# Hybrid encoder layer, convolution stages: own bytes for the raw memory weights, second-stage loads written first, a third buffer in the last stage

## The chip, the cores and the metric

The kernel runs on one core of a Trainium2 chip. The metric is the device time of one execution in microseconds (us), the median of several runs. TensorE runs the matrix products; VectorE, ScalarE and GpSimd do the element-wise work; SyncE (SP) issues nearly all transfers between DRAM and the core's on-chip memory, in one queue, which 16 DMA engines work off.

## What is computed

One layer on two sequences (4096 and 1024 rows of 1024 values) that share their weights:

```python
h = rms_norm(x, norm_in)
z = h @ w_in                      # columns for the three branches and a gate
y_hy  = x0 * (fft_conv(x1 * v, filter) + skip * x1 * v)
y_att = dilated_attention(q, k, v, rel_bias)      # 6 heads, 3 window sizes
y_mem = memory_attention(qm, mem, mem_norm, w_mem_kv, ...)   # 4 heads, 256 memory rows
x + (concat(y_hy, y_att, y_mem) * silu(gate)) @ w_out
```

The change touches two parts of it: the long convolution `fft_conv`, and the preparation of `w_mem_kv`, the weights from which the keys and values of the memory rows are made.

## The kernel before

Products are run as three half-precision products each (`mm3`, lines 275 to 282: high by high, high by low, low by high), so each weight is scaled by a power of two and split into a high and a low part (`wsplit`, lines 235 to 264: load, multiply by a gain on GpSimd, largest magnitude on VectorE, high part on ScalarE, low part on VectorE).

`phases` (line 1586) first runs the projection for the convolution branch (`hyena_proj`, its weights in `wh`, its products in `zh`). Then it weaves two streams. `dense` makes the queries, keys and values row block by row block (`qkv`, products `z` from `wA` and a row block `hA`, three at a time) and then the gates. `side` runs `long_conv` for both sequences, then `memory_kv`, then the attention. Each generator yields an estimated cost, and `weave` takes the next piece from the stream that has spent less; a bare yield such as `IDLE_2` lets the dense stream run for so long. `K_C` = 1.35 scales the costs of `long_conv`, and `IDLE_2` is 9000 and 16000 (ns) for the two sequences.

The order of TensorE's instructions is the order in which the program writes them. On the other engines and on the queue of SP the scheduler places each instruction by its estimate of when it is ready, and among ready ones by a priority that rises in the order of writing, with the dense stream (3 million) ahead of the side stream (4 million). On each engine the result is one list that is worked off in order.

`long_conv` (line 1231) is a Fourier convolution in three stages, each in a pool of its own:

- `pc1`: the scaled signal is split into `s16` from pieces `sl` of 1024 columns (lines 1248 to 1258); `conv_stage1` transposes 64 (16) blocks of it on TensorE (line 1282), multiplies by a constant matrix and stores the result to `as_d` in DRAM (line 1298).
- `pmw`, for the first sequence only: `memory_weights` (line 503) loads the four parts of `w_mem_kv` in two pairs, into two buffers of 4 KB a partition, and writes the split weights `wm` into a pool that stays. It has no matmul. Its products with the memory rows come in `memory_kv`, some 580 us later.
- `pc2`: `conv_stage2` loads batches of four groups (`fk` from the filter's spectrum `as_k`, `fa` from `as_d`, constant matrices `mt`; the first batch of the first sequence is one group), makes spectra (line 1335 and line 1352), multiplies them, and transforms back (line 1376) into `bs` in DRAM.
- `pc3`: `conv_stage3` loads eight blocks at a time from `bs` into `bt` (line 1403, two buffers; for the first sequence eight batches in two transfers of 768 KB each, for the second two batches), runs 24 small matmuls for each of three channel groups (line 1420), and ScalarE writes them to `big` (line 1425).

A pool takes the bytes above the pools that are open. When it closes, the next pool takes the same bytes, and its tiles wait until the tiles that lay there are no longer in use. So before the change `pc1`, `pmw`, `pc2` and `pc3` all begin at the same byte.

Of the kernel before, what the change touches and what calls it, by code (L numbers as in the profile page):

```python
# [12 lines left out]
F32 = mybir.dt.float32  # L13
F32R = mybir.dt.float32r
F16 = mybir.dt.float16
I32 = mybir.dt.int32
AF = mybir.ActivationFunctionType
ALU = mybir.AluOpType
# [4 lines left out]
P = 128  # L23
# [115 lines left out]
K_C, IDLE_1, IDLE_2, IDLE_3, IDLE_M = 1.35, (34000, 28000), (9000, 16000), 18000, 40000  # L139
# [39 lines left out]
class Layer:  # L179
# [1051 lines left out]
    def long_conv(self, ps, i, mpool):  # L1231
        nc, x = self.nc, self.x
        L = self.seqs[i][1]
        NB, q = self.groups_of(i)
        nb = L // 512
        m = self.const.tile([P, 3, 4], F32, name=f"lm{i}")
        nc.vector.tensor_reduce(out=m[:, :, 0:1], in_=self.smax[i], axis=AX.X, op=ALU.max)
        nc.vector.tensor_scalar_max(m[:, :, 0:1], m[:, :, 0:1], 1e-30)
        self.pow2(m[:, :, 1:2], m[:, :, 0:1])
        nc.vector.tensor_scalar_mul(m[:, :, 1:2], m[:, :, 1:2], 2.0)  # L1240
        nc.vector.reciprocal(m[:, :, 2:3], m[:, :, 1:2])
        nc.vector.scalar_tensor_tensor(
            out=m[:, :, 3:4], in0=m[:, :, 1:2], scalar=1.0 / (128.0 * NB * 0.5 / 16.0), in1=self.rn[i][:, 1:4].unsqueeze(2),
            op0=ALU.mult, op1=ALU.mult,
        )
        with self.pool("pc1") as sub:
            s16 = sub.tile([P, 3, 2 * L], F16, name="s16", bufs=1)
            for t0 in range(0, L, 1024):
                for c in range(3):
                    sv = s16[:, c].rearrange("p (a l) -> p a l", a=2)  # L1250
                    t = sub.tile([P, 1024], F32, tag="sl", name="sl", bufs=2)
                    self.ld(t, self.s_d[i][c, :, t0:t0 + 1024])
                    nc.scalar.activation(out=sv[:, 0, t0:t0 + 1024], in_=t, func=AF.Identity, scale=m[:, c, 2:3])
                    nc.vector.scalar_tensor_tensor(
                        out=sv[:, 1, t0:t0 + 1024], in0=t, scalar=m[:, c, 2:3], in1=sv[:, 0, t0:t0 + 1024],
                        op0=ALU.mult, op1=ALU.subtract,
                    )
                    yield 800
            yield IDLE_1[i]
            yield from self.conv_stage1(sub, ps, i, s16)  # L1260
        if mpool is not None:
            with self.pool("pmw") as wpool:
                self.memory_weights(mpool, wpool)
        yield IDLE_2[i]
        with self.pool("pc2") as sub:
            yield from self.conv_stage2(sub, ps, i)
        yield IDLE_3
        with self.pool("pc3") as sub:
            big = sub.tile([P, 3, L], F32, name="big", bufs=1)
            yield from self.conv_stage3(sub, ps, i, big, m)  # L1270
# [28 lines left out]

        yield from pipe(NB, (2, stage1), (0, turn))  # L1300

    def conv_stage2(self, pool, ps, i):

        nc, x = self.nc, self.x
        NB, q = self.groups_of(i)
# [9 lines left out]
        def load(nb):  # L1315
            g0, n = batches[nb]
            w = loaded[nb] = {}
            w["k"] = self.load_stage(pool, i, self.as_d[i, "k"], g0, n, "fk2", 4)
            w["x"] = self.load_stage(pool, i, self.as_d[i], g0, n, "fa2", 4)
            w["m"] = pool.tile([P, 4, 2, 2, P], F16, tag="mt", name="mt", bufs=MT)  # L1320
            self.ld(w["m"][:, :n], x[f"mats{i}"][g0:g0 + n].rearrange("g p (m a b) -> p g m a b", m=2, a=2))

        load(0)

        def spectrum(g):
            nb, j = where[g]
            if j == 0 and nb + 1 < len(batches):
                load(nb + 1)
            w = loaded[nb]
            kr = slice(0, 64) if (q == 1 and g in (0, 64)) else slice(0, P)  # L1330
            kt = kts[g] = pool.tile([P, 2, DH], F32, tag="kt", name="kt", bufs=3)
            kp = ps.tile([P, 512], F32, tag="e", name="kp", bufs=2)
            for nn, (ml, ah) in enumerate(PASSES):
                hs = slice(ah * DH, (ah + 1) * DH)
                nc.tensor.matmul(
                    kp[:, :DH], w["m"][kr, j, 0, ml, :], w["k"][kr, j, hs], start=(nn == 0), stop=(nn == 2)
                )
            yield 490
            for a, b in ((0, 0), (0, 1), (1, 1)):
                nc.scalar.activation(  # L1340
                    out=kt[64 * b:64 * b + 64, a], in_=kp[64 * a:64 * a + 64, :DH], func=AF.Identity,
                    scale=rn[64 * a:64 * a + 64, 0:1],
                )
# [51 lines left out]
    def conv_stage3(self, pool, ps, i, out, m):  # L1395
        nc = self.nc
        L = self.seqs[i][1]
        NB, q = self.groups_of(i)
        bs = self.bs[i]
        nbat = 8  # L1400

        def load(n0):
            bt = pool.tile([P, nbat, 768], F16, tag="bt", name="bt", bufs=2)
            nk = 64 // q
            for ri in range(2):
                for l in range(q):
                    p0, r0 = 64 * ri + nk * l, 2 * NB * l + NB * ri + n0
                    self.ld(bt[p0:p0 + nk], bs[r0:r0 + nbat, 0:nk].rearrange("n k c -> k n c"))
            return bt

        nxt = load(0)
        for n0 in range(0, NB, nbat):
            bt = nxt
            if n0 + nbat < NB:
                nxt = load(n0 + nbat)
            for c in range(3):
                o = ps.tile([P, nbat, 64], F32, tag="f", name="o", bufs=3)
                for jn in range(nbat):
                    for nn, (dh, ch) in enumerate(((0, 0), (0, 1), (1, 0))):
                        nc.tensor.matmul(  # L1420
                            o[:, jn, :], bt[:, jn, dh * DH + c * P:dh * DH + (c + 1) * P], self.cinv[i][:, ch, :],
                            start=(nn == 0), stop=(nn == 2),
                        )
                yield 24 * 44
                nc.scalar.activation(
                    out=out[:, c, :L].rearrange("p (n t) -> p t n", t=NB)[:, n0:n0 + nbat, :], in_=o,
                    func=AF.Identity, scale=m[:, c, 3:4],
                )
        self.st(self.cv[i].rearrange("c p l -> p c l"), out[:, :, :L])
# [251 lines left out]
```

## Time and profile before

| | |
|---|---|
| median of the runs | 3072.31 us (3069.44 to 3073.78, 3 runs) |
| profiled execution | 3067.02 us, of it 3065.2 us span |
| TensorE busy | 2775.0 us, 91% of the span |
| VectorE busy | 2052.3 us, 67% |
| ScalarE busy | 1663.4 us, 54% |
| GpSimd busy | 1259.7 us, 41% |
| DMA | 610.38 MB, mean 199 GB/s |

The span runs from the first to the last instruction. A busy TensorE is not one at its peak, since overlapping matmuls count in full. In a row of the timeline the brackets hold the idle time of the engine ahead of the instruction and what ended it; an `x24` folds 24 alike instructions.

### The profile page before, as it was taken

The page shows a single profiled execution, that of the slowest core. Times are in us where ns is not written, and L with a number is a line of the kernel's source. Part 1 is how long each engine was busy: PE and PEld are TensorE (multiplying, and loading weights), DVE is VectorE, ACT ScalarE, POOL GpSimd, SP SyncE. Part 2 cuts the span into 40 slices and gives each one's busy share as a digit, 9 for nine tenths or more (in the row PEclk, how much of TensorE's full clock was granted, in tenths as well). Part 3 has the DMA queues.
Part 4 walks back from the last instruction along what each step waited for, and adds up shares of the span by engine and source line. Part 5 has one row for each costly group of instructions (what it writes and reads, how often), then busy time and mean ns, then how long its engine had stood idle before and what let it go on. Part 6 is the DMA issues. An engine that isn't in the chain of part 4 may idle for free. (4 is left out here: it accounts for less than half of the span.)

```text
span 3065.2 us, 55390 instructions
## 1 busy us (share of the span) xinstructions
PE 2775.0 (91%) x19620; PEld 1725.3 (56%) x19620; DVE 2052.3 (67%) x5237; ACT 1663.4 (54%) x3149; POOL 1259.7 (41%) x1534
## 2 busy tenths in 40 slices
PE   5998989888959998999999998989899899999999
PEld 2444444333625544544456666666666665778787
DVE  7777888787648882364567666767677665665663
ACT  5666666334738884464366565656566554232321
POOL 2336777232126661142133233333344344555551
PEclk9999999999979999999999999999999999999999
DMA  7554444555559969697499999999998989777762
GB/s 224 175 151 151 155 148 146 155 164 190 208 167 230 246 200 209 214 202 176 110 222 265 216 202 203 225 210 191 210 219 197 202 172 315 250 239 252 236 223 97
DMA packets 761855, 610.38 MB, mean 199 GB/s; under 512 B 514958, under 2 KB 702262, under 8 KB 758122
## 3 DMA queue, kind: packets, MB, share of 16 engines
q1 hardware_dynamic: 761578, 606.84, 75.2%
q8 instruction: 155, 2.54, 0.3%
q14 instruction: 122, 1.00, 0.1%
HBM read 289.08 MB, written 199.92 MB: 160 GB/s over the span
## 5 line engine op out<-in xcount | busy, mean ns | idle before, releaser
L1063 ACT ACTIVATE pt<-pt,nm 128x256 f32<-128x256 f32 (+2 forms) x880 | 350.0, 472 | 182.6 <-DVE nm L1061 171.4
L279 PE MATMUL z<-wA,hA 128*128 128x512 f16 (+1 forms) x960 | 352.5, 367 | 18.1 <-ACT rw L440 14.5
L280 PE MATMUL z<-wA,hA 128*128 128x512 f16 (+1 forms) x960 | 352.7, 367 | 0.0
L281 PE MATMUL z<-wA,hA 128*128 128x512 f16 (+1 forms) x960 | 352.5, 367 | 0.0
L1051 DVE CUSTOM_DVE_ANT_0 pt<-s,tab,lsc 128x256 f32<-128x256 f32 (+1 forms) x672 | 278.9, 449 | 100.9 <-PE s L1047 89.5
L279 PE MATMUL zh<-hB,wh 128*128 128x512 f16 x720 | 280.1, 389 | 25.0 <-ACT zb L877 24.8
L280 PE MATMUL zh<-hB,wh 128*128 128x512 f16 x720 | 279.5, 388 | 1.5 <-DVE hB L384 1.5
L281 PE MATMUL zh<-hB,wh 128*128 128x512 f16 x720 | 279.3, 388 | 0.0
L279 PE MATMUL oo<-wo,mhi 128*128 128x512 f32 x640 | 257.3, 402 | 10.1 <-DVE xr L1557 5.0
L281 PE MATMUL oo<-wo,mlo 128*128 128x512 f32 x640 | 253.8, 397 | 1.3 <-POOL mlo L1536 1.3
L280 PE MATMUL oo<-wo,mhi 128*128 128x512 f32 x640 | 253.7, 396 | 0.0
L1079 POOL CAST hl<-pt 128x256 f16<-128x256 f32 (+1 forms) x212 | 102.8, 499 | 359.4 <-ACT pt L1063 288.3
L279 PE MATMUL zg<-hG,wg 128*128 128x512 f16 x640 | 246.9, 386 | 0.8 <-DVE vr L475 0.7
L280 PE MATMUL zg<-hG,wg 128*128 128x512 f16 x640 | 246.8, 386 | 0.0
L281 PE MATMUL zg<-hG,wg 128*128 128x512 f16 x640 | 246.1, 385 | 0.0
L1099 DVE TENSOR_TENSOR tl<-tt,th 128x512 f16<-128x512 f32 (+1 forms) x280 | 187.8, 673 | 59.9 <-ACT th L1098 58.4
L1098 ACT ACTIVATE th<-tt 128x512 f16<-128x512 f32 (+1 forms) x280 | 159.4, 574 | 102.5 <-PE yp L1120 50.3
L1094 PE MATMUL tt<-ident,pt 128*128 128x128 f32 x1088 | 173.4, 282 | 35.6 <-DVE tl L1099 25.8
L1044 PE MATMUL s<-kT,qT 128*128 128x256 f16 (+2 forms) x720 | 165.6, 261 | 38.2 <-DVE mx L1051 33.9
L1080 POOL TENSOR_TENSOR hl<-pt,hl 128x256 f16<-128x256 f32 (+1 forms) x212 | 190.4, 906 | 6.4
L891 DVE SCALAR_TENSOR_TENSOR u<-zb,cw,u 128x512 f32<-128x512 f32 (+2 forms) x180 | 167.3, 933 | 33.4 <-ACT u L887 29.9
L1094 PEld LDWEIGHTS tt<-ident,pt 128*128 128x128 f32 x1088 | 132.1, 145 | 71.3 <-issue 31.3
(303 smaller groups left out, 7167.7 us busy)
## 6 DMA issues: line engine op xcount, KB each, us to landing
y<-yc SPq DMA_DIRECT2D x120, 198.0 KB, 4.5
yc<-y SPq DMA_DIRECT2D x112, 198.0 KB, 2.8
xt<-in_x SPq DMA_DIRECT2D x40, 512.0 KB, 4.7
hts<-hB SPq DMA_DIRECT2D x10, 2048.0 KB, 6.6
hA<-hts SPq DMA_DIRECT2D x40, 512.0 KB, 5.4
rows<-rw SPq DMA_DIRECT2D x40, 512.0 KB, 4.3
hG<-hts SPq DMA_DIRECT2D x10, 2048.0 KB
gt<-go SPq DMA_DIRECT2D x80, 256.0 KB, 3.3
```

What stands on the lines that cost most here:

```text
L279: nc.tensor.matmul(out, pick_l(lh, k), pick_r(rh, k), start=(k == 0), stop=False)
L280: nc.tensor.matmul(out, pick_l(lh, k), pick_r(rl, k), start=False, stop=False)
L281: nc.tensor.matmul(out, pick_l(ll, k), pick_r(rh, k), start=False, stop=(k == n - 1))
L891: nc.vector.scalar_tensor_tensor(out=u[:, :w], in0=zb[:, c0 + d:c1 + d], scalar=cw[:, j, tap:tap + 1], in1=u[:, :w], op0=ALU.mult, op1=ALU ...
L1044: nc.tensor.matmul(s[:, a, :W], g["qT"][:, h, qs], g["kT"][:, h, kc:kc + W], start=True, stop=False,)
L1051: nc.vector.tensor_tensor_reduce(out=pt[:, h, :W], in0=s[:, a, :W], in1=zero.to_broadcast([P, NMEM]) if mem else tb[:, h, t0:t0 + W], scal ...
L1063: nc.scalar.activation(out=pt[:, h, :W], in_=pt[:, h, :W], func=AF.Exp, bias=nm[:, h:h + 1])
L1079: nc.gpsimd.tensor_copy(hl[:, 0, :, c], src)
L1080: nc.gpsimd.tensor_tensor(out=hl[:, 1, :, c], in0=src, in1=hl[:, 0, :, c], op=ALU.subtract)
L1094: nc.tensor.transpose(tt[:, a, ci, :], pt[:, 2 * pr + a, w0:w0 + P], self.ident)
L1098: nc.scalar.activation(out=th[:, :, :n], in_=tt[:, :, :n], func=AF.Copy)
L1099: nc.vector.tensor_tensor(out=tl[:, :, :n], in0=tt[:, :, :n], in1=th[:, :, :n], op=ALU.subtract)
```

## The change

`pmw` is opened ahead of `pc1` and closed after `pc2`, so the buffers of the raw memory weights lie below both, and `pc1` and `pc2` share bytes among themselves alone. `conv_stage2` loads its first batch, then calls `memory_weights`, then yields `IDLE_2`; before, the weights and the yield stood ahead of the pool. The costs that are yielded, and their order, are the same. `conv_stage3` has three buffers `bt` and loads two batches before the first product and batch n + 2 at batch n.

```diff
-        with self.pool("pc1") as sub:
-            s16 = sub.tile([P, 3, 2 * L], F16, name="s16", bufs=1)
...
-            yield IDLE_1[i]
-            yield from self.conv_stage1(sub, ps, i, s16)
-        if mpool is not None:
-            with self.pool("pmw") as wpool:
-                self.memory_weights(mpool, wpool)
-        yield IDLE_2[i]
-        with self.pool("pc2") as sub:
-            yield from self.conv_stage2(sub, ps, i)
+        with self.pool("pmw") as wpool:
+            with self.pool("pc1") as sub:
+                s16 = sub.tile([P, 3, 2 * L], F16, name="s16", bufs=1)
...
+                yield IDLE_1[i]
+                yield from self.conv_stage1(sub, ps, i, s16)
+            with self.pool("pc2") as sub:
+                yield from self.conv_stage2(
+                    sub, ps, i, IDLE_2[i], (lambda: self.memory_weights(mpool, wpool)) if mpool is not None else None
+                )
...
-    def conv_stage2(self, pool, ps, i):
+    def conv_stage2(self, pool, ps, i, idle, aside):
...
         load(0)
+        if aside is not None:
+            aside()
+        yield idle
...
-            bt = pool.tile([P, nbat, 768], F16, tag="bt", name="bt", bufs=2)
+            bt = pool.tile([P, nbat, 768], F16, tag="bt", name="bt", bufs=3)
...
-        nxt = load(0)
+        bts = [load(n0) for n0 in range(0, min(2 * nbat, NB), nbat)]
         for n0 in range(0, NB, nbat):
-            bt = nxt
-            if n0 + nbat < NB:
-                nxt = load(n0 + nbat)
+            bt = bts.pop(0)
+            if n0 + 2 * nbat < NB:
+                bts.append(load(n0 + 2 * nbat))
```

## Rows read from the trace of the kernel before

**Rows 1.** Waits of TensorE, 873:935 and 1165:1250: us in total, times, longest.
```profile
PE kp L1335 <- DMA mt<-in_mats: 33.8, 2, 28.9
...
PE o L1420 <- DMA bt<-bs: 15.6, 4, 5.8
```

**Rows 2.** Timeline of TensorE: start, duration, instruction, idle before it and its releaser.
```profile
902.08 1.14 PE L1335 MATMUL kp<-fk,mt 64*128 64x384 f16 x3 [28.86 <-DMA mt<-in_mats]
...
912.04 1.14 PE L1335 MATMUL kp<-fk,mt 128*128 128x384 f16 x3 [4.96 <-DMA mt<-in_mats]
...
916.95 0.38 PE L279 MATMUL z<-wA,hA 128*128 128x512 f16 x1
```

**Rows 3.** Stretches: length, busy time (instructions) of five engines, TensorE clock, DMA share, GB/s.
```profile
872.85:902.08 29.23, 0.38 (x2) 0.00 (x1) 18.78 (x57) 5.79 (x7) 7.43 (x6) 0.54 0.29 91
902.08:916.95 14.87, 9.91 (x27) 3.22 (x28) 3.06 (x6) 3.98 (x7) 1.90 (x2) 0.52 1.10 242
916.95:919.22 2.27, 2.27 (x14) 1.18 (x12) 1.10 (x3) 2.00 (x4) 0.99 (x1) 1.00 1.10 213
```

**Rows 4.** Timeline of the DMA issues on SP, 858:935.
```profile
861.41 0.32 SPq L195 DMA_DIRECT2D as_d<-av  x1
861.82 1.70 SPq L192 DMA_DIRECT2D ws<-in_w_mem_kv  x2
...
898.62 0.49 SPq L192 DMA_DIRECT2D fk<-as_k  x1
...
900.42 1.29 SPq L192 DMA_DIRECT2D fk<-as_k  x2
```

**Rows 5.** Timeline of VectorE and of ScalarE in the memory weights' chain.
```profile
871.34 1.22 DVE L249 TENSOR_REDUCE peak<-ws 128x1 f32<-128x1024 f32 x1 [9.88 <-POOL ws L248]
...
894.64 2.19 ACT L260 ACTIVATE wm<-ws,wsa 128x1024 f16<-128x1024 f32 x2 [11.96 <-DVE wsa L257]
```

**Rows 6.** DMA issues, 840:870: count, size, median us to landing.
```profile
vrows<-vr SPq DMA_DIRECT2D x1, 193.5 KB, 6.1
```

**Rows 7.** A setup load on SP's timeline; the first projection's products (durations, first, last).
```profile
19.41 1.93 SPq L192 DMA_DIRECT2D gains<-in_att_q_norm  x1
...
L281 PE MATMUL zh<-hB,wh x720: 377/379/634, 40.5 to 697.6; 128*128 128x512 f16 x180
```

**Rows 8.** Stretches ahead of stage 1 of the first sequence.
```profile
700.00:770.00 70.00, 58.71 (x281) 28.13 (x280) 52.98 (x117) 30.76 (x42) 16.22 (x18) 0.95 0.57 185
...
705.00:710.00 5.00, 4.50 (x21) 1.96 (x20) 4.26 (x19) 1.15 (x1) 1.04 (x1) 1.00 0.00 0
```

**Rows 9.** Last split of s16 on VectorE's timeline; the transposes of s16 (first start).
```profile
767.58 1.28 DVE L1254 SCALAR_TENSOR_TENSOR s<-sl,lm,s 128x1024 f16<-128x1024 f32 x1
...
L1282 PE MATMUL tp<-ident,s x240: 218/251/314, 772.5 to 1303.7; 128*128 128x128 f16 x120
```

**Rows 10.** Timeline of the DMA issues on SP: second sequence's second stage.
```profile
1306.75 5.44 SPq L192 DMA_DIRECT2D fk<-as_k  x8
```

**Rows 11.** Timeline of TensorE in stage 3, a restart after a wait.
```profile
1218.28 1.44 PE L1420 MATMUL o<-cinv,bt 128*128 128x64 f16 x24 [4.41 <-DMA bt<-bs]
...
1223.36 0.99 PE L1420 MATMUL o<-cinv,bt 128*128 128x64 f16 x24
```

**Rows 12.** Stretches of 5 us in stage 3 of the first sequence.
```profile
1165.00:1170.00 5.00, 5.00 (x25) 2.29 (x24) 0.82 (x1) 2.14 (x3) 0.26 (x1) 1.00 1.13 203
1170.00:1175.00 5.00, 5.00 (x69) 3.24 (x67) 1.59 (x2) 2.50 (x4) 0.87 (x2) 1.00 0.46 142
1175.00:1180.00 5.00, 5.00 (x70) 3.37 (x69) 3.10 (x9) 3.63 (x6) 1.15 (x2) 1.00 0.57 188
...
1205.00:1210.00 5.00, 5.00 (x80) 3.64 (x79) 3.37 (x9) 3.59 (x7) 0.00 (x0) 1.00 0.48 101
```

**Rows 13.** Timeline of the DMA issues on SP in stage 3.
```profile
1161.89 0.33 SPq L192 DMA_DIRECT2D hA<-hts  x1
...
1176.79 1.26 SPq L192 DMA_DIRECT2D bt<-bs  x2
```

More of the change, by code (lines that the diff above doesn't have):

```diff
@@ L1245, in long_conv @@
         )
-        with self.pool("pc1") as sub:
-            s16 = sub.tile([P, 3, 2 * L], F16, name="s16", bufs=1)
[L1248 to L1258, printed above, removed]
-            yield IDLE_1[i]
-            yield from self.conv_stage1(sub, ps, i, s16)
-        if mpool is not None:
-            with self.pool("pmw") as wpool:
-                self.memory_weights(mpool, wpool)
-        yield IDLE_2[i]
-        with self.pool("pc2") as sub:
-            yield from self.conv_stage2(sub, ps, i)
+        with self.pool("pmw") as wpool:
+            with self.pool("pc1") as sub:
+                s16 = sub.tile([P, 3, 2 * L], F16, name="s16", bufs=1)
+                for t0 in range(0, L, 1024):
+                    for c in range(3):
+                        sv = s16[:, c].rearrange("p (a l) -> p a l", a=2)
+                        t = sub.tile([P, 1024], F32, tag="sl", name="sl", bufs=2)
+                        self.ld(t, self.s_d[i][c, :, t0:t0 + 1024])
+                        nc.scalar.activation(out=sv[:, 0, t0:t0 + 1024], in_=t, func=AF.Identity, scale=m[:, c, 2:3])
+                        nc.vector.scalar_tensor_tensor(
+                            out=sv[:, 1, t0:t0 + 1024], in0=t, scalar=m[:, c, 2:3], in1=sv[:, 0, t0:t0 + 1024],
+                            op0=ALU.mult, op1=ALU.subtract,
+                        )
+                        yield 800
+                yield IDLE_1[i]
[3 more added lines that the diff above has]
+                    sub, ps, i, IDLE_2[i], (lambda: self.memory_weights(mpool, wpool)) if mpool is not None else None
+                )
         yield IDLE_3
```

## The prediction

> **What bounds the kernel now.** I read part 2 of the page first: TensorE is at nine tenths in nearly every one of the 40 slices, and the dips that lie in one stage each are what a local edit can fill. Then the waits of TensorE in the two stretches that the diff touches [rows 1]: 33.8 us for the constant matrices of the first transform's second stage, in two waits, and 15.6 us for its third stage, in four. TensorE runs in the order in which the program is written, and the edit writes no matmul in another place, since the memory weights have none. So the chain of TensorE is the same list of instructions before and after, and only the waits in it can change.
>
> The first dip, read in the timeline of TensorE [rows 2]: the last dense matmul starts at 872.85, the first spectrum matmul of stage 2 at 902.08 after 28.86 us of idle. Another 4.96 us follow ahead of the second spectrum. The stretch table [rows 3] shows that nothing was busy for its own sake: the DMA engines were at 0.29 in the gap. From 902.08 to 916.95 the granted clock was 0.52, that is mostly the lower level of 1.2 GHz, after an idle of 28.9 us. The queue of the DMA issues [rows 4] says why: the memory weights are loaded at 861.82, as soon as stage 1 has left the bytes, and the first load of stage 2 (fk) is issued at 898.62, after the last split of the weights. Their chain runs through DMA, GpSimd, VectorE and ScalarE one after another, with waits of 9.88 us on VectorE and 11.96 us on ScalarE in it [rows 5]. Stage 2 waits for bytes, not for data.
>
> **Part 1: bytes of their own for the raw memory weights.** After the edit `fk`, `fa` and `mt` stand on the bytes of stage 1 only. Two things hold them then: the last reading of `s16`, over by 861.82, when the weights were let onto the same bytes, and the last store of stage 1, issued at 861.41 [rows 4]. The nearest row for that store's landing is 6.1 us, from a store of `vrows` in the same stretch [rows 6], so `fa` can be issued at about 867.5. TensorE wants it at about 874.2, the matrices at 873.1.
>
> What goes: 28.86 us of idle. Then the stretch of 14.87 us [rows 3]: it holds nine groups of three matmuls (five on the spectra, four dense). At the full clock four such groups take 2.27 us, the last row of [rows 3], so the nine take about 5.1. The loss there is 9.8 us, 4.96 of it the second wait and 4.8 the low clock. Together 38.7 us.
>
> What is next late there: the load of the second batch. In the trace before, its first DMA is issued at 900.42 and the spectrum that needs it starts at 912.04: 11.6 us [rows 2, 4]. Now it can be issued from about 861 to 868, so it lands between 873 and 880; it is wanted at 875.4 (matrices) to 876.5 (product). I take 1.5 us of wait; the bounds are nothing and the whole 9.8 us of before.
>
> **Where the memory weights go.** Engines other than TensorE, and the DMA queue, take what is ready. The gains of the setup are issued at 19.41, though they are written behind a yield of 50 us of TensorE's time [rows 7]. So the weights, once they wait for no bytes of stage 1, will go as soon as the bytes of the first pool are left: its weights are last read at 697.6 [rows 7]. At 705 to 710 the DMA share was 0.00 [rows 8], so the first pair loads free. The work itself is most of the 18.8 us of VectorE, 5.8 of ScalarE and 7.4 of GpSimd in the old gap [rows 3]. It then lies beside the preparation of `s16`, in a stretch where VectorE has 17 of 70 us free and TensorE idles 11 [rows 8]. `s16` is complete at 768.9 and first read at 772.5 [rows 9], a cover of 3.6 us. The second pair of loads (1 MB) must share the DMA engines with the loads of `s16`, and GpSimd, VectorE and ScalarE work in order, so an eviction of a dense product can stand behind a weight that has not arrived. I take 2 us on TensorE. Bounds: below nothing there is no reason for a gain; above, see the last rival.
>
> **Part 2: the load of stage 2 is written ahead of its yield.** For the second sequence this is all that changes, and it is worth nothing: its loads went out at 1306.75 already, as soon as its stage 1 was over [rows 10], because the yield orders TensorE alone. Nor does writing them ahead of the weights matter by itself: what held them was the bytes.
>
> **Part 3: the third buffer of stage 3.** The second sequence has two batches and loads both ahead in either version: nothing. For the first, four waits sum to 15.6 us [rows 1], and after the longer ones TensorE restarts at the lower clock: from 1218.28 to 1223.36 it needs 5.08 us [rows 11] for 24 small matmuls and 9 dense ones, which take 0.70 + 9 x 0.2155 = 2.64 at the full clock. That is 2.4 us; for three such restarts I take 6. So 21.5 us are lost there. But the third buffer gives back only what the DMA engines left unused. While they carried `bt` they were at a share of 1.13 and 203 GB/s [rows 12]; a batch (two DMAs of 768 KB) takes 7.75 us of them at that rate, and TensorE eats one in 6 to 7 us. They fell to 0.46 and 0.57 at 1170 to 1180, when both buffers were full and the next load waited for 1176.79 [rows 12, 13], and to 0.48 at 1205 to 1210. Set against 1.13 that is 5 x (0.67 + 0.56 + 0.65) / 1.13 = 8.3 us of transfer. So the last batch arrives some 8 us sooner, and TensorE keeps about 13 of the 21.5. I take 8; the bounds are 3 (if the dense stream's block `hA`, issued at 1161.89 [rows 13] behind six instead of four transfers, comes late for the next tile) and 21.5.
>
> The Trainium skill, "DMA: Bandwidth & Descriptors", section "Bandwidth", measures 341 GB/s for a transfer of 1 MB. By that figure a batch would take an estimated 4.6 us, the stage would be TensorE's and all 21.5 us would come back; the trace's 203 GB/s, with descriptors of 1.5 KB, speaks against it.
>
> **Sum.** -38.7 + 1.5 + 2 - 8 = -43.2 us. The profiled execution took 3067.02 us (span 3065.2) and would take 3024; it lies 5.3 us below the median of the runs, 3072.31, and I carry the difference to that median: 3029. It should pass to the end whole, since TensorE's list behind 916.95 is the same and its loads are set off by its own progress. That orders on the other engines shift a little everywhere is an uncertainty of some 10 us either way that no row prices.
>
> **Rivals.**
> - The weights do not move ahead but stay at about 862 to 900, now beside stage 2. For: they are written there, with the lowest rank of the two streams. Against: the gains at 19.41. ScalarE is then the bound: at the full rate of stage 2 it is busy 2.00 of 2.27 us [rows 3], so the weights' activations (most of 5.8 us) come on top, and a wait of up to 11.96 us at its head [rows 5] stops the evictions behind it. Then 38.7 shrinks to 21 to 33, and with 8 less 1.5 the whole gain is 27 to 39: 3033 to 3045, about 3038.
> - Stage 3 gives back everything. For: the first two batches were in, and the engines at half their share, before TensorE had emptied a buffer [rows 12]. Against: the share of 1.13 ahead of that. 38.7 - 1.5 - 2 + 21.5 = 56.7: 3016.
> - The stall moves instead of going, and the kernel is slower: the weights' chain, now ahead of stage 1, holds up `s16`. If all of the chain's engine time (18.8 + 5.8 + 7.4) and its two long waits (21.8) came in front of `s16`, the first transpose would be late by 53.8 - 3.6 = 50.2 us, with 4.8 of low clock behind it: 55 against a gain of 45, so 3082. It decides from the point where `s16` is complete later than about 817 instead of 768.9. For: VectorE is three quarters busy there and works in order. Against: the weights rank below `s16`, and most of that work lies on different engines at the same time.
> - The same with part of it (s16 complete between 808 and 820), or loads of stage 2 still held by something I do not see: no change, about 3070.
>
> **How the numbers follow.** Forecast 0.60, weights beside stage 2 0.20, all of stage 3 0.10, no change 0.05, slower 0.05. The likeliest gives 3029. The range must leave out no more than 0.2: 3012 (nothing new late, all of stage 3 back, -60) to 3052 (weights in the way at their worst, 3 us from stage 3, and something over). Faster than 0.2% (about what a measurement of this kernel tells from no change, 6 us) 0.90, within it 0.05, slower 0.05.
>
> **What would show it.** Right: no wait of the first spectrum over 3 us, at about 873; a granted clock of 1.00 through it; `ws<-in_w_mem_kv` issued near 700 and not at 861; waits of stage 3 down to some 10 us with the DMA share near 1.1 throughout; stage 2 to the end the same length. Wrong: the first transpose of stage 1 later than 776; waits of ScalarE for the weights' scales inside stage 2; stage 3 without a wait, or with as many.

## The result, and the profile after

The changed kernel takes 3045.19 us in the median (3033.4 to 3053.22, 6 runs), the kernel before 3070.88 us beside it (3063.98 to 3080.76). The ratio is 0.9914, with a 95% interval of 0.9894 to 0.9935: by the ratio 26.4 us less (20 to 33 by the interval; the medians differ by 25.7), where 43 were forecast. A second series of runs gives 0.9906 (0.9884 to 0.9929). The profiled execution of the changed kernel took 3053.22 us (span 3051.3), the slowest of its six.

Line numbers from 1254 on are shifted by up to 3 against before (transposes L1281, spectrum L1337, product L1354, stage 3 L1422).

The waits of TensorE for transfers at the beginning of stage 2 and in stage 3 of the changed kernel (columns as in [rows 1]):

```profile
PE kp L1337 <- DMA mt<-in_mats: 3.9, 1, 3.9
...
PE o L1422 <- DMA bt<-bs: 8.2, 3, 4.3
```

And its timeline, the first spectra and product (columns as in [rows 2]):

```profile
885.68 0.66 PE L1337 MATMUL kp<-fk,mt 64*128 64x384 f16 x3
887.02 0.66 PE L1354 MATMUL xp<-fa,mt 64*128 64x384 f16 x3
892.32 1.14 PE L1337 MATMUL kp<-fk,mt 128*128 128x384 f16 x3 [3.88 <-DMA mt<-in_mats]
...
897.44 0.38 PE L279 MATMUL z<-wA,hA 128*128 128x512 f16 x1
```

The wait of 28.86 us [rows 2] is gone; the second spectrum still waits. But the first spectrum starts at 885.68 and not at the 873 at which the dense work was through before. The stretch table (columns as in [rows 3]) shows what the second wait leaves behind it: a clock of 0.76, a mixture of the two levels, with the DMA engines now at a share of 1.08. The nine groups that took 14.87 us before [rows 3] take 11.8 here, from 885.68 to 897.44.

```profile
885.00:895.00 10.00, 6.12 (x24) 2.15 (x23) 5.31 (x8) 4.74 (x8) 3.44 (x3) 0.76 1.08 296
```

SP's queue, start and duration of each issue, against [rows 4]:

```profile
716.42 1.02 SPq L192 DMA_DIRECT2D ws<-in_w_mem_kv  x2
...
750.45 3.42 SPq L192 DMA_DIRECT2D ws<-in_w_mem_kv  x2
...
873.94 0.32 SPq L195 DMA_DIRECT2D as_d<-av  x1
874.35 0.48 SPq L192 DMA_DIRECT2D fk<-as_k  x1
878.71 0.46 SPq L192 DMA_DIRECT2D fa<-as_d  x1
879.22 0.58 SPq L192 DMA_DIRECT2D mt<-in_mats  x1
879.85 1.29 SPq L192 DMA_DIRECT2D fk<-as_k  x2
881.18 1.27 SPq L192 DMA_DIRECT2D fa<-as_d  x2
```

The raw weights moved ahead as forecast, from 861.82 to 716.42 and 750.45. The first `fk` follows stage 1's last store by 0.4 us, so nothing holds the bytes any more. Then the queue stands still for 4 us: the first `fa` reads what that store writes, and while it waits to be issued, `mt` and the whole second batch stand behind it, though of these only the second `fa` reads what stage 1 wrote.

What the weights did where they are now, in the stretch from 720 to 780: first the kernel before,

```profile
720.00:780.00 60.00, 49.87 (x248) 24.57 (x247) 48.95 (x113) 29.52 (x43) 13.37 (x14) 0.97 0.62 201
```

then the changed one,

```profile
720.00:780.00 60.00, 49.40 (x234) 23.42 (x232) 58.28 (x123) 28.90 (x37) 21.05 (x15) 0.94 0.67 214
```

then a kernel without the weights' work (`e_no_weights`, below):

```profile
720.00:780.00 60.00, 49.26 (x229) 23.43 (x228) 48.10 (x110) 26.94 (x38) 11.72 (x12) 0.91 0.61 197
```

VectorE (the third busy time) is full: 58.28 of 60 us. The last split of `s16` starts 10 us later than before [rows 9]:

```profile
777.68 1.27 DVE L1255 SCALAR_TENSOR_TENSOR s<-sl,lm,s 128x1024 f16<-128x1024 f32 x1
```

It is still complete 1.6 us before the first transpose, and TensorE shows no wait for it. But that transpose is now at 780.5 instead of 772.5. Of these 8 us 3.7 are there already when the first projection ends (701.3 against 697.6 [rows 7]); in `e_after`, whose first projection ends at 697.6 too, it comes at 778.8. TensorE's dense products ahead of it wait longer for their evictions by VectorE, and stage 1 behind it waits for VectorE too. In the changed kernel, from the first projection's end to the first spectrum, the waits of TensorE that involve VectorE are these:

```profile
PE z L279 <- DVE vr L475: 8.7, 3, 3.8
PE a L1291 <- DVE av L1295: 6.1, 6, 2.3
```

Before, they were 2.6 and 1.5 us. The waits for ScalarE in the same stretch fell from 13.1 to 8.3 us, so that all waits of TensorE there, without the stall, grew from 17.2 to 23.3 us. The stages between landmarks of TensorE, from the first and last starts of its groups, in us; each row is one profiled execution:

| kernel | last `zh` to first `kp` | to first `o` | to last `tp` (second sequence) | to last `z` of `wA` | to last `oo` |
|---|---|---|---|---|---|
| before | 204.5 | 270.0 | 131.6 | 334.1 | 1422.7 |
| `e_before` | 207.7 | 269.5 | 131.7 | 336.8 | 1433.0 |
| after | 184.4 | 268.0 | 121.0 | 335.8 | 1436.1 |
| `e_after` | 190.1 | 268.4 | 121.7 | 335.4 | 1444.9 |
| `e_own_bytes` | 189.3 | 266.6 | 131.1 | 336.7 | 1433.2 |
| `e_third_buf` | 204.8 | 269.4 | 121.5 | 332.3 | 1434.7 |
| `e_weights_late` | 178.3 | 280.5 | 121.0 | 336.3 | 1426.7 |
| `e_mats_first` | 189.3 | 265.5 | 120.6 | 332.4 | 1438.5 |
| `e_weights_seq2` | 178.1 | 268.2 | 132.6 | 332.0 | 1430.7 |
| `e_no_weights` | 181.8 | 266.6 | 120.1 | 336.4 | 1434.6 |
| `e_no_gain` | 188.1 | 265.3 | 121.2 | 333.4 | 1428.6 |
| `e_no_low` | 184.8 | 266.3 | 121.4 | 330.2 | 1432.4 |
| `e_half_bt` | 190.0 | 268.0 | 109.2 | 330.6 | 1425.2 |
| `e_best` | 178.0 | 266.4 | 121.0 | 349.5 | 1425.1 |

The second column is stage 2 of the first sequence, the third its stage 3 and the second sequence's transposes, the fourth the rest of the second sequence and the dense products, the last attention, gates and output.

### The profile page after: what moved, and what is told of

The parts are those of the page before. It is cut to its first block, busy times and chain, and to the rows that moved or that the text cites. A ratio compares the mean times of both kernels' runs of the same rounds, so it can differ in the third digit from the quotient of the medians.

```text
span 3051.3 us, 55381 instructions
## 1 busy us (share of the span) xinstructions
PE 2787.6 (91%) x19620; PEld 1730.6 (57%) x19620; DVE 2054.2 (67%) x5237; ACT 1663.9 (55%) x3149; POOL 1263.1 (41%) x1534
## 4 chain that ended last, share of the span: by engine, by line
PE 37%; DVE 16%; DMA 16%; ACT 7%; issue 6%; POOL 4%; SPq 2%; DVEq 0%; ACTq 0%; POOLq 0%
DMA qT<-rows 5%; PE zg L279 3%; PE zg L280 3%; PE z L279 3%; PE z L280 3%; PE zg L281 3%; PE z L281 3%; PE tt L1094 3%; PE oo L281 2%; PE oo L279 2%; PE oo L280 2%; PE s L1044 2%; DMA gg<-gt 1%; DVE qS L969 1%; PE s L1047 1%
## 5 line engine op out<-in xcount | busy, mean ns | idle before, releaser
L1063 ACT ACTIVATE pt<-pt,nm 128x256 f32<-128x256 f32 (+2 forms) x880 | 350.0, 472 | 187.6 <-DVE nm L1061 178.3
L1094 PE MATMUL tt<-ident,pt 128*128 128x128 f32 x1088 | 172.8, 281 | 40.7 <-DVE tl L1099 29.3
```

What stands on the lines that cost most here:

```text
L1063: nc.scalar.activation(out=pt[:, h, :W], in_=pt[:, h, :W], func=AF.Exp, bias=nm[:, h:h + 1])
L1094: nc.tensor.transpose(tt[:, a, ci, :], pt[:, 2 * pr + a, w0:w0 + P], self.ident)
```

## The experiments

The theory after the first traces: two separate gains (the stall of stage 2, the third buffer), and two givings-back (the weights ahead of stage 1, the second batch behind `fa`). The rivals: that the gains are one, that attention gives some of it back, and that other causes hold the second batch and stage 3.

**The changed kernel once more.** No edit.

> The changed kernel once more, unchanged, for what repeats. In the first trace of the change the work up to the last dense product was 27 us ahead of before, but the stretch from the last dense product z to the last gate product zg took 951.1 us against 936.8. Theory (scatter): that execution was the slowest of its six (3053 against a median of 3045), and the 14 us are its own; here the stretch takes 935 to 944 us and the whole about 3045. Rival (order): the change moves instructions of the other engines in the attention, so the stretch takes about 950 again, whatever the whole time is. Both expect the first spectrum of stage 2 without a wait at about 886, the second with a wait of some 4 us, and stage 3 at about 121 us from its first product to the last transpose of the second sequence.

Measured: 3050.84 us against 3081.77, ratio 0.9906 (0.9884 to 0.9929). The stretch from the last dense product to the last gate product took 959.2 us, longer than both said. Its own execution took 3064.57 us, 14 above its median. So this trace doesn't separate the two; the one of `e_before`, below, does better. The wait ahead of the second spectrum (4.2 us) and stage 3 (121.7) repeat.

**The parts apart.** First own bytes alone, then the third buffer alone:

```diff
-            bt = pool.tile([P, nbat, 768], F16, tag="bt", name="bt", bufs=3)
+            bt = pool.tile([P, nbat, 768], F16, tag="bt", name="bt", bufs=2)
...
-            if n0 + 2 * nbat < NB:
-                bts.append(load(n0 + 2 * nbat))
+            if n0 + nbat < NB:
+                nxt = load(n0 + nbat)
```

> Own bytes for the raw weights and the loads written first, but two buffers in stage 3 as before. Theory (two separate gains): the stall of stage 2 goes as in the changed kernel (32 us there, 9 given back ahead of it by the weights beside the preparation of s16 and stage 1), stage 3 waits four times for some 15 us again and takes about 131 us; 3070.9 - 32 + 9 + 5 for the scatter between traces = 3048 to 3055. Rival (one gain): stage 3 ran faster because it began earlier against the dense stream, not for its buffer; then stage 3 takes about 121 us with two buffers and the time is 3045.

Measured: 3058.4 us against 3081.77, ratio 0.9927 (0.991 to 0.9945); stage 3 took 131.1 us. Then the same lines the other way round, on the kernel before:

> The third buffer of stage 3 alone, on the kernel before. Theory (two separate gains): the stall of 28.9 us ahead of stage 2 stays, stage 3 has waits of about 8 us instead of 15.6, the time is 8 to 10 us less, 3061 to 3063. Rival (one gain): nothing that can be measured, 3069 to 3072, with stage 3 at about 131 us.

Measured: 3068.3 us against the same 3081.77, ratio 0.9962 (0.9946 to 0.9978); stage 3 took 121.5 us, the stall stayed (204.8). The gains are two, 22 and 12 us by the ratios (29 for both together in the same series), and stage 3's is the buffer's. In stage 3 the third buffer does what was said: it keeps the DMA engines at work. The stretch of 30 us from the 14th us of the stage on, in `e_own_bytes` with two buffers,

```profile
1168.00:1198.00 30.00, 20.35 (x279) 13.10 (x279) 5.13 (x11) 13.57 (x16) 2.68 (x3) 0.89 1.00 203
```

and in the changed kernel with three:

```profile
1167.00:1197.00 30.00, 25.72 (x353) 16.34 (x350) 5.13 (x11) 17.30 (x22) 2.67 (x3) 0.94 1.10 227
```

**The weights beside stage 2.** Their pool opens after stage 1's has closed:

```diff
-        with self.pool("pmw") as wpool:
-            with self.pool("pc1") as sub:
...
+        with self.pool("pc1") as sub:
...
+        with self.pool("pmw") as wpool:
             with self.pool("pc2") as sub:
```

> As the changed kernel, but the raw weights' pool is opened after stage 1's pool is closed and stage 2's pool above it: the weights wait for stage 1 again, while stage 2 waits for no bytes of theirs. So they lie beside stage 2 instead of beside s16 and stage 1. Theory A (what the weights cost comes from where they lie: VectorE is slowed and busy ahead of s16): the last dense products and the first transposes come 4 us earlier, stage 1 takes 100 us instead of 105, first spectrum at about 877, stage 2 has room for them: about 3036. Theory B (the rival of the forecast: ScalarE bounds stage 2 and works in order, so the weights cost there 6 to 18 us): about 3042 to 3054, with waits of TensorE inside stage 2 for evictions.

Measured: 3048.43 us, ratio 0.989 (0.9873 to 0.9908), the changed kernel's within the scatter. Both theories were half right. Ahead of stage 2 the gain is as theory A has it (178.3), and stage 2 gives it back as theory B has it: 280.5 us against 267.7 (the mean of after, `e_after` and `e_own_bytes`). The rows are 30-us stretches of stage 2 from its 30th and 60th us on, of `e_after`:

```profile
917.00:947.00 30.00, 29.37 (x164) 15.85 (x163) 25.26 (x48) 25.20 (x50) 17.71 (x19) 1.00 0.94 246
947.00:977.00 30.00, 29.69 (x162) 15.71 (x161) 26.11 (x48) 24.76 (x49) 18.43 (x20) 1.00 0.92 241
```

and of `e_weights_late`:

```profile
907.00:937.00 30.00, 25.94 (x141) 13.58 (x139) 26.94 (x58) 21.95 (x42) 19.48 (x20) 1.00 0.91 212
937.00:967.00 30.00, 26.86 (x148) 14.46 (x148) 26.83 (x48) 25.51 (x49) 19.29 (x20) 1.00 0.90 241
```

In the first of them, with the weights there, ScalarE is less busy than without the weights (21.95 against 25.20), VectorE more. But busy time does not show who waits. TensorE's waits for ScalarE's evictions of the spectra, which theory B named, are these in stage 2 of `e_after`,

```profile
PE kp L1337 <- ACT kt L1342: 0.9, 2, 0.5
```

and of `e_weights_late`:

```profile
PE kp L1337 <- ACT kt L1342: 5.7, 4, 3.6
```

The longest, 3.6 us, ends at 938.16, behind two of the weights' activations on ScalarE (933.87, 2.17 us). So 4.8 of the 12.8 us are theory B's. The waits for VectorE grew by 3.7 us, and the wait for `mt` at the stage's head is 7.9 us instead of 4.2, with the first pair of the weights' loads ahead of the second batch in SP's queue.

**The kernel before once more.** No edit.

> The kernel before once more, for its trace. Its first trace took 936.8 us from the last dense product z to the last gate product zg; the five kernels with a part of the change took 942.7 to 959.2 there. Theory (scatter): that stretch differs between executions of one kernel by over 10 us, since waits and granted clock feed each other in it; here it takes 942 to 955. Rival (order): instructions of the other engines are ordered differently in the attention once the convolution is shorter, which costs some 10 us; here 935 to 939 again. Stage 3 takes 131 us, the stall of stage 2 28 to 30, in both.

Measured: 948.2 us in that stretch, where the first trace had 936.8; 3079.37 us in the median. It scatters by over 10 us in one and the same kernel. The largest wait of TensorE from 1640 to 2560 in the first trace of before,

```profile
PE s L1044 <- DVE mx L1051: 28.1, 19, 3.8
```

and in `e_before`, the same wait, longer:

```profile
PE s L1044 <- DVE mx L1051: 34.6, 22, 5.9
```

So the 14 us that the changed kernel's first trace loses there are within what executions of one kernel differ by. That a part is due to a changed order is not excluded: the three traces with the weights ahead and three buffers and all work done (951.1, 959.2, 953.6 in `e_mats_first`) are the longest, while `e_half_bt`, which differs from them in stage 3 alone, took 943.1. The medians show no such loss: `e_after` was 29.2 us ahead of `e_before` at the last dense product, and its median is some 30 us below before's.

**Matrices and filter first.**

```diff
+        load_km(0)
+        load_km(1)
         load(0)
```

with `load_km` the part of `load` for `fk` and `mt`, and `load` left with `fa` where that is done.

> As the changed kernel, but the filter's part fk and the constant matrices of the first two batches are issued ahead of the first fa. In the trace of the change the first fa stands at the head of SP's queue for some 4 us until stage 1's last store has landed, and the second batch's fk and mt stand behind it; TensorE waits 3.88 us for mt ahead of the second spectrum and runs some 9 us at a lower clock behind it. Theory (head of the queue): the wait goes and with it the clock, some 6 us of the stretch from first to tenth spectrum; 4 to 6 us faster than the changed kernel beside it. Rival (bytes on the DMA engines): the second batch, 1 MB and more, just takes so long; the wait moves from the matrices to fa ahead of the second product, and the time stays.

Measured: 3046.75 us against 3079.53, ratio 0.9898 (0.9882 to 0.9914); the interval holds the changed kernel's ratio, so a gain of 2 to 4 us in the whole is not shown. The trace shows where it would come from. TensorE's first spectra and products on the timeline,

```profile
888.32 0.66 PE L1344 MATMUL kp<-fk,mt 64*128 64x384 f16 x3
889.66 0.66 PE L1361 MATMUL xp<-fa,mt 64*128 64x384 f16 x3
890.91 0.65 PE L1344 MATMUL kp<-fk,mt 128*128 128x384 f16 x3
893.53 0.65 PE L1361 MATMUL xp<-fa,mt 128*128 128x384 f16 x3 [1.32 <-DMA fa<-as_d]
```

and the 10 us from the first on:

```profile
888.00:898.00 10.00, 8.68 (x44) 3.79 (x43) 8.04 (x12) 7.35 (x13) 5.34 (x5) 1.00 1.09 265
```

The wait of 3.88 us is gone and the clock stays at 1.00; 1.32 us come back as a wait for `fa`, and 1.9 for the third batch. The nine groups take 6.8 us instead of 11.8. So the place in the queue was the cause of the second spectrum's wait, as the theory said, and the rival was right on a part: with a DMA share of 1.09 the batches come late for the next reader. That the stage as a whole is shorter by it is not shown: it takes 265.5 us against 267.7, but `e_no_gain`, without this edit and with a wait of 3.4 us in the old place, took 265.3.

**The weights in the second sequence.**

```diff
-                        yield from scaled(self.long_conv(ps, i, mpool if i == 0 else None), K_C)
+                        yield from scaled(self.long_conv(ps, i, mpool if i == last else None), K_C)
```

> As the changed kernel, but the memory weights are made in the second sequence's convolution; their bytes are those of the first sequence's third stage, so they go at about 1250 to 1290, beside the second sequence's s16 and transposes. With the weights beside stage 1 (the changed kernel) the stretch from the last product of the first projection to the first product of stage 3 took 452 and 458 us, beside stage 2 459, where before took 474.5 with the stall in it. Theory A (the weights cost 9 to 12 us wherever VectorE, GpSimd and ScalarE already have work): that stretch falls to 443 to 448, and the same 9 to 12 us come back between 1240 and 1300; no difference. Theory B (they cost only where the side stream waits for the same engines): the second sequence's convolution has long dense stretches between its stages, so most of 9 to 12 us stays gained.

Measured: 3049.33 us, ratio 0.9901 (0.9887 to 0.9915). From the last `zh` to the first `o` it took 446.3 us (178.1 + 268.2), and the next stretch 132.6 instead of 121: theory A, in both halves.

**Without the weights.**

```diff
-        for j in (0, 2):
-            self.wsplit(...)
+        nc.vector.memset(S[:, 0:4], 1.0)
+        for k in range(KC):
+            nc.gpsimd.memset(wm[:, k], 1.0)
```

> As the changed kernel, but the memory weights are not made: no loads, no multiply by the gain, no magnitudes, no split; GpSimd writes ones into their place in eight pieces. The output is then another. It gives the whole price of the weights' work in the changed kernel. Theory (they delay s16 and stage 1): the stretch from the last product of the first projection to the first spectrum takes 175 to 178 us instead of 184 to 190, the time is 8 to 12 us less than the changed kernel. Rival (the stretch is bound by the loads of s16 and by VectorE's other work): 2 us or less.

Measured: 3044.0 us, ratio 0.9887 (0.987 to 0.9904). First spectrum after 181.8 us; three kernels with the weights elsewhere show 178.0 to 178.3, five with them ahead and untouched 184.4 to 190.1, 188.6 in the mean. The price of the weights ahead of stage 2 is thus 7 to 10.5 us, by the landmarks; the ratio (some 6 us less than `e_after`'s) doesn't contradict it and can't confirm it. 181.8 is longer than the theory's 175 to 178; why it isn't 178, with no weights at all, stays open.

**Two cuts into the weights' work.** First GpSimd's multiplication:

```diff
-                self.g_mem, tag="wms", bufs=2,
+                None, tag="wms", bufs=2,
```

> As the changed kernel, but the memory weights are not multiplied by the norm's gain: GpSimd's four multiplications of a part (3.75 to 5.06 us each) are left out, and loads, magnitudes and split stay. It asks why the weights cost 8 to 12 us ahead of the first spectrum. In the trace of the change VectorE's instructions beside GpSimd's multiplication are longer (4.08 instead of 2.44 us for two splits of s16, 4.49 instead of some 0.55 for three small ones). Theory (the two engines slow each other): VectorE's long ones go, the first spectrum is at 880 to 883 instead of 886 to 888. Rival (it is VectorE's and ScalarE's own work for the weights, some 17 and 5 us, in order ahead of evictions): 885 to 888 again.

Measured: ratio 0.9907 (0.9886 to 0.9929); first spectrum after 188.1 us (at 883.5, with the first projection's end 2.2 us earlier than in `e_after`). The expectation's 5.06 us are of a pair of multiplications; single ones take 1.89 to 3.02 in the changed kernel. Then VectorE's low halves:

```diff
+            if tag == "wms":
+                nc.scalar.activation(out=dlo, in_=dhi, func=AF.Copy)
+                continue
```

> As the changed kernel, but the low halves of the memory weights are not computed on VectorE (eight instructions of 0.65 to 2.39 us); ScalarE copies the high halves into their place (four activations of some 1.1 us), so the output is another. The multiplication on GpSimd, the magnitudes and all loads stay. Five kernels with the weights ahead of stage 1 took 184.4 to 190.1 us from the last product of the first projection to the first spectrum, three with the weights elsewhere 178.0 to 178.3; leaving out the multiplication on GpSimd gave 188.1. Theory (VectorE is full: 58.3 of the 60 us from 720 to 780, against 49.0 before, and its surplus is what stage 1 waits for): that stretch takes 180 to 184 us, and the waits of TensorE in stage 1 for VectorE's part of av fall from 6 to 10 us to under 4. Rival (GpSimd's chain, the loads or the order decide): 187 to 190 again.

Measured: ratio 0.9906 (0.9885 to 0.9928), 184.8 us, with waits of 5.7 us for `av`, not under 4. VectorE was busy 55.22 of the 60 us:

```profile
720.00:780.00 60.00, 49.47 (x235) 23.73 (x234) 55.22 (x126) 34.16 (x47) 21.31 (x15) 0.94 0.71 219
```

Neither decides. 184.8 is just outside what the theory said, 188.1 inside the rival's range, and the same kernel gave 184.4 and 190.1. That the weights' work costs 7 to 10.5 us is shown; how it divides into VectorE's time, the slowing of VectorE by GpSimd and the order on each engine stays open.

**Half the bytes in stage 3.**

```diff
-            bt = pool.tile([P, nbat, 768], F16, tag="bt", name="bt", bufs=3)
+            bt = pool.tile([P, nbat // 2, 768], F16, tag="bt", name="bt", bufs=3)
...
-                            o[:, jn, :], bt[:, jn, dh * DH + ...
+                            o[:, jn, :], bt[:, jn // 2, dh * DH + ...
```

> As the changed kernel, but each load of stage 3 brings four blocks instead of eight, and the products use each block twice: half the bytes, the same matmuls, another output. It asks what the rest of stage 3's waits is. With three buffers TensorE still waits 8 to 9 us for bt, with the DMA engines at a share of 1.05 to 1.12 throughout and 200 to 220 GB/s. Theory (the transfers' time is what is left, and the third buffer could give no more): all waits for bt go, the stretch from the first product of stage 3 to the last transpose of the second sequence takes 107 to 112 us instead of 121. Rival (a delay at each load, by the queue or the buffers' turn): waits of over 5 us stay.

Measured: 3022.74 us against 3071.64, ratio 0.9831 (0.9807 to 0.9856). Stage 3 has no wait for `bt` left and takes 109.2 us; TensorE is busy throughout:

```profile
1169.00:1199.00 30.00, 30.00 (x438) 19.61 (x437) 5.13 (x11) 20.91 (x25) 2.68 (x3) 1.00 0.61 147
```

The theory holds: what three buffers leave is transfer time.

**A version from these.** Three buffers, `load_km` first, and the weights in the second sequence with their pool between stage 1 and stage 2, that is, the diffs of `e_weights_late`, `e_mats_first` and `e_weights_seq2` together.

> A version made of what the runs showed: third buffer; fk and matrices of the first two batches ahead of the first fa; and the memory weights made in the second sequence after its stage 1, on its stage 1's bytes, so that they lie at about 1276 to 1310, beside a stretch of dense work in which the convolution has little to do, and not beside s16, stage 1 or a stage 2 of 129 spectra. Theory (the weights' price is paid only beside the side stream's own work): the last product of the first projection to the first of stage 3 takes 443 to 447 us (452 to 459 in the changed kernel), stage 3 121, the second sequence's convolution no longer than 137, and the time is 8 to 12 us less than the changed kernel's, some 3038 to 3042 beside a before of 3080. Rival (they are paid anywhere, as at 1250 to 1290, where stage 3 and the second s16 took 132.6 instead of 121): the 9 us come back in the second sequence's stages, 3046 to 3050.

Measured: 3044.35 us against 3071.64, ratio 0.9916 (0.9898 to 0.9934): no better than the changed kernel. The first sequence took what the theory said (178.0 + 266.4 + 121.0), and the second gave it back: 349.5 us against 330 to 337 in all others. The rows are a stretch of the second sequence's stage 2, in `e_after`

```profile
1340.00:1360.00 20.00, 20.00 (x114) 10.89 (x113) 16.86 (x33) 18.35 (x37) 13.08 (x14) 1.00 0.58 185
```

and in `e_best`:

```profile
1340.00:1360.00 20.00, 14.07 (x72) 7.46 (x72) 19.56 (x39) 17.36 (x30) 9.67 (x11) 0.91 0.25 95
```

VectorE is full again (19.56 of 20), and TensorE waits. The 9 us came back, as the rival said. But the weights did not come to lie where the theory wanted them. The second sequence's spectra and the weights' last splits in `e_best`,

```profile
L1344 PE MATMUL kp<-fk,mt x51: 323/326/524, 1286.6 to 1360.5; 128*128 128x384 f16 x51
...
L262 DVE SCALAR_TENSOR_TENSOR wm<-ws,wsa,wm x8: 739/748/1487, 1314.2 to 1354.5; 128x512 f16<-128x512 f32 x8
```

and the spectra in `e_after`:

```profile
L1337 PE MATMUL kp<-fk,mt x51: 326/326/524, 1301.2 to 1360.5; 128*128 128x384 f16 x51
```

The weights' loads went out at 1285 and 1318, and their splits lie at 1314 to 1355, in the middle of the second sequence's stage 2, which took 73.9 us instead of 59.3. So this run gives a fourth price beside the side stream's own work; that the weights would cost less beside dense work alone was not tested. In the four places tried they cost 7 to 16 us, and no version here beats the changed kernel by more than the runs can tell.

## Why the forecast came out as it did

The time lies in the range, 16 us above the predicted value, and the direction and the two mechanisms were right. Step by step, forecast beside what the landmarks show (means of before, `e_before` and `e_third_buf` against the kernels named):

| term | forecast | measured | from |
|---|---|---|---|
| the stall ahead of the first spectrum | -28.9 | -27.6 | 205.7 to 178.1 (`e_weights_late`, `e_weights_seq2`, `e_best`) |
| second spectrum's wait and low clock | -9.8 + 1.5 | -1.9 | 269.6 to 267.7 (after, `e_after`, `e_own_bytes`) |
| weights ahead of stage 1 | +2 | +10.5 | 178.1 to 188.6 (after, `e_after`, `e_own_bytes`, `e_mats_first`, `e_half_bt`) |
| third buffer | -8 | -10.3 | 131.5 (before, `e_before`, `e_own_bytes`) to 121.2 (after, `e_after`, `e_mats_first`, `e_third_buf`) |
| sum | -43.2 | -29.3 | |

The difference is 13.9 us: 8.5 from the weights and 6.4 from the second batch, 1.3 from the stall, less 2.3 from the third buffer. The measured sum of -29.3 is 3 us from the ratio's -26.4 and inside its interval. The two large misses add up instead of cancelling. The range held because its upper end was drawn for the weights in the way and for only 3 us from stage 3; stage 3 gave 10, so that it held is luck in part.

**What held the bytes** was read rightly: the first wait went, `fk` is issued right behind the last store, and the weights went to the first free bytes, as the gains at 19.41 had suggested [rows 7]. The rival "weights stay beside stage 2" did not occur by itself; made by hand (`e_weights_late`) it costs 12.8 us in stage 2, about what did occur (10.5), and in part by the waits for ScalarE that it named.

**The weights' price** is the term most mis-sized. The step that failed is "where VectorE has 17 of 70 us free": the same sentences gave the work as most of 18.8 us of VectorE. 53.0 and most of 18.8 come to about 70, so by the forecast's own rows [rows 3, 8] VectorE had to become full. It did, at 58.28 of 60 us, and the term of 2 us measured 7 to 10.5. I looked at the cover of `s16` (3.6 us) and not at what else stands in VectorE's queue: the evictions of the dense products, and those of stage 1 behind them. The forecast named the sign that this had happened, a first transpose later than 776; it came at 780.5, and at 778.8 in `e_after`. The slower rival had the weights in the way at the size of the whole chain, 50.2 us; a fifth of that came, and not by a wait for `s16`, which it named. That the price goes by way of VectorE's queue is argued from its busy time and from the waits for `vr` and `av`; the two cuts leave it open.

**The second batch** was estimated by when its bytes are free ("it can be issued from about 861 to 868"). That `fa` waits for the store's landing was in the working; that `mt` and the second batch stand behind `fa` in one queue was not, and `e_mats_first` shows that this made the wait. The load was issued 5.9 us behind the last store, at the late end of the forecast's "861 to 868"; landed at its 880 and wanted at its 875.4, it gives 4.6 us by the forecast's own numbers, and 3.88 were measured. The term also left out that the clock falls behind such a wait, though [rows 3] showed it: the nine groups took 11.8 us where 5.1 + 1.5 were forecast. By these groups alone the gain is 3.1 us, by the whole stage 1.9.

**The third buffer** was right in mechanism and nearly in size. The estimate of 21.5 us for all that stage 3 loses also stands: with half the bytes the stretch fell by 22.4 us (131.6 to 109.2), of which the buffer gives 10.3 and transfer time keeps the rest. That "all of stage 3 comes back" is thereby refuted for the full bytes. By the estimate from the figure of the Trainium skill, "DMA: Bandwidth & Descriptors", section "Bandwidth" (341 GB/s for 1 MB, measured on transfers issued from GpSimd), all would have come back; here, with loads issued from SP, the 227 GB/s at a share of 1.10 decide against it.

**To the end**: the medians are consistent with the difference passing whole (29.2 us at the last dense product, `e_after` against `e_before`, and 30.9 between the medians of `e_after` and of the kernel before beside it); in single traces the attention differs by 11 us in one kernel (936.8 and 948.2) and by 22 over all, which hides any part of 10 us there.

## What to carry to other kernels

When work that is off the path is freed from a wait, add its engine time to the busy time of the stretch to which it will move, engine by engine; if the sum comes near the stretch, suspect that the wait was hiding a price that now has to be paid. Here it was paid in each of four places, all of them beside other work of the same stream. A load that reads what has just been stored held the queue for 4 us here, with everything behind it: put first what depends on nothing. Another buffer gave back about what the transfer engines had left idle, which the stretch table shows beforehand (8 us by the table, 10.3 measured).

## What the runs showed of the hardware

VectorE and GpSimd slow each other more than I had thought of. Three copies of 32 x 32 values on VectorE lasted 4.49 us beside GpSimd's work, most of it two multiplications of the memory weights; four of them took 0.72 us in the same trace. Of the two multiplications the first lasted 3.02 us, beside a split of `s16` (1.27 us) that had begun just ahead of it; in the kernel before all four took 1.89. GpSimd's timeline in the changed kernel,

```profile
758.63 4.87 POOL L248 TENSOR_TENSOR ws<-ws,g_mem 128x1024 f32<-128x1024 f32 x2
```

and VectorE's:

```profile
737.34 0.72 DVE L225 COPY peaks<-peak 32x32 f32<-32x32 f32 x4
...
758.62 1.27 DVE L1255 SCALAR_TENSOR_TENSOR s<-sl,lm,s 128x1024 f16<-128x1024 f32 x1
759.92 4.49 DVE L225 COPY peaks<-peak 32x32 f32<-32x32 f32 x3
764.44 1.22 DVE L486 TENSOR_REDUCE hv<-rw 128x16 f32<-128x1024 f32 x1
```

Busy time of VectorE in such a stretch is thus not all work. The Trainium skill, "SBUF — State Buffer", section "Who interferes with whom", says that the two engines share a port pair, and that where an instruction of VectorE uses both of its port pairs, the engine that came first holds the shared one for its whole instruction while the other is blocked. These rows agree: the first copy ends at about 761.7 and the second at 763.5, as the two multiplications do, and the third at 764.4 with GpSimd's next product. How much of the weights' 7 to 10.5 us it is, the runs leave open.

The DMA engines moved twice as much at about the same share in another stretch. In `e_after`, 5 us of `bt` (rows of 1.5 KB) and 5 us after the store of `big` (rows of 16 KB, and in the other direction) was issued:

```profile
1184.00:1189.00 5.00, 2.96 (x30) 2.13 (x31) 0.00 (x1) 1.13 (x1) 0.99 (x1) 0.69 1.12 206
...
1225.00:1230.00 5.00, 5.00 (x28) 2.52 (x27) 0.49 (x1) 1.08 (x2) 0.00 (x0) 1.00 1.01 433
```
